# Weight loads of the recurrent stretch moved from SyncE's DMA queue to GpSimd's

## The chip, the cores and the metric

The kernel runs on one core of a Trainium2 chip. The metric is the device time of one launch in microseconds (us); lower is better. The engines are named as in the profile: PE (matmul), PEld (the weight load into PE), DVE (VectorE), ACT (ScalarE), POOL (GpSimd) and SP (SyncE, which here only issues DMAs). A name with a q behind it (SPq, ACTq) is the engine's DMA-issuing instructions.

## The reference, cut to what matters

One inference step of a two-layer decoder, for a prompt of 1024 tokens and 8 samples of 8 tokens, width 1024, all in float32:

```python
for i in range(DEPTH):                       # 2 layers
    h, gate = ada_norm(x, c, ...)            # RMS norm with shift, scale and gate from c
    o = stick_breaking(h) if i == 0 else rwkv7(h)
    x = x + gate * (o @ w_o)
    h, gate = ada_norm(x, c, ...)
    x = x + gate * (square(relu(h @ w_up)) @ w_down)     # hidden width 4096

# rwkv7: r, k, v = three 1024x1024 products; decay w, a, g by small low-rank products; then per head
def step(S, inp):
    sa = einsum('bhij,bhj->bhi', S, kk_t)
    S = S * w_t - sa * b_t + v_t * k_t
    return S, einsum('bhij,bhj->bhi', S, r_t)
```

## The kernel before

**Halves.** The 1088 tokens are two halves, A (576 columns, all prompt) and B (448 prompt columns and the 64 sample columns). A dense product of one half is the foreground; attention, and later the recurrence, is a background stream of generators whose steps are put between the matmuls (`step`, `behind`, `beside`). The order of the recurrent part is: first norm of the recurrent layer for A (`rw_norm`), `mixer_in(0)` with the products by `rw_w_r`, `rw_w_k` and `rw_w_v`; then for B the attention's `sb_w_o`, the first layer's MLP (`w_up`, `w_down` in eight blocks), `rw_norm` and `mixer_in(1)`; then for A `rw_w_o` and the last MLP; then the same for B.

**Weights.** `weight` brings one weight tile at a time: a DMA into the stage tile `wst` (three buffers; 512 KB, or 256 KB for `w_down`), a rounded copy `wh` by ACT (L350) and the remainder `wl` by DVE (L351), three buffers each. `dense` then runs three matmuls for each 128 rows (L364 to L366): `wh` by the high part of the operand, `wh` by its low part, `wl` by the high part. A load into `wst` waits until DVE has read the tile three loads earlier (L351). L347 is the line of that DMA. It goes to ACT's queue while the samples' attention runs (`sampling`), and to SP's queue otherwise.

**The recurrence.** For each half and each of eight pairs of heads, `rw_unit` (L1082 on) loads `k` and `r`, prepares the chunk matrices and stores them (`s_st`, `s_l`); on POOL it has the operations L1105 (`G`), L1108, L1119, L1120 (`a`) and L1130 (`AR`). `rw_lanes` loads `llt` (L1207), inverts small triangular blocks on DVE (L1216, L1218) and stores `s_tt` and `s_xn` (L1223, L1226). `rw_chain` then loads `st`, `tt`, `Lq`, `x` and `hv` (L1262 to L1274) and walks the chunks in two rows at once (`qc`, `invq`). `rw_out` normalises the result (POOL: L1465, L1482, L1498). Most stores of `rw_unit` and `rw_value` (`s_st`, `s_l`, `s_p`, `s_v`) go to ACT's queue; all loads go to SP's.

**Order.** The order of the instructions of each engine is set when the kernel is built: a scheduler plays the program through with times of its own, and each engine's queue gets the order that comes out. On the chip each queue runs in that order; an instruction whose semaphores are not there yet holds all behind it on its engine.

The rest of POOL's work in this part: the one-column copies `prod` (L552) of the attention's carry, the low parts `xlo` and `slo` of every other operand tile (L311), and, for B, the 64 sample columns of the norms (L302 to L304) and of the residual (L385).

Of the kernel before, what the change touches and what calls it, by code (L numbers as in the profile page):

```python
# [106 lines left out]
class Kern:  # L107
# [35 lines left out]
    def setup(self, ctx):  # L143
        nc, tc, I = self.nc, self.tc, self.I
        self.misc = ctx.enter_context(tc.tile_pool(name="misc", bufs=1))
        self.dram = ctx.enter_context(tc.tile_pool(name="scr", bufs=1, space=DRAM))
        cst = self.misc.tile([128, C_N], F32, name="cst")
        nc.sync.dma_start(cst, I["consts"])
        self.cst = cst
        self.ident = cst[:, C_ID:C_ID + 128]  # L150
        self.ones32 = self.misc.tile([128, 32], F32, name="ones32")
        nc.vector.memset(self.ones32, 1.0)
        self.sampling = False
        self.behind(iter(()))
        self.side = iter(())
        self.beside(iter(()), 0.0)
        self.eps = self.misc.tile([128, 1], F32, name="eps")
        nc.vector.memset(self.eps, EPS)
# [99 lines left out]
    def rms(self, x, pt, tmp, ps, tag, slot, rslot=None):  # L258

        for R in self.rms_steps(x, pt, tmp, ps, tag, slot, rslot):  # L260
            pass
        return R

    def rms_steps(self, x, pt, tmp, ps, tag, slot, rslot=None):
# [19 lines left out]
        nc.vector.tensor_mul(r, y, t)  # L284
        R = tmp.tile([128, W], F32, tag=rslot or slot, name="R", bufs=2 if rslot else None)
        for g in range(4):
            qb = ps.tile([128, 512], F32, tag=tag, name="rb")
            nc.tensor.matmul(qb[:, :w], self.cst[:, C_SELB + 128 * g:C_SELB + 128 * g + 128], r,
                             start=True, stop=True)
            self.copy(R[:, w * g:w * g + w], qb[:, :w])  # L290
        yield R

    def modulate(self, s, f, x, R, pt, t):

        nc = self.nc
        mod = self.mod[s]
        P, S = slice(0, pt.NP), slice(pt.NP, pt.W)
        nc.vector.scalar_tensor_tensor(t[:, P], x[f][:, P], mod[:, 8 + f, 0:1], R[:, P], ALU.mult,
                                       ALU.mult)
        if pt.NP < pt.W:  # L300
            ts = t[:, S].rearrange("p (b t) -> p b t", b=8)
            nc.gpsimd.tensor_mul(t[:, S], x[f][:, S], R[:, S])  # L302
            nc.gpsimd.tensor_mul(ts, ts, mod[:, 8 + f, 1:9].unsqueeze(2).to_broadcast([128, 8, 8]))
            nc.gpsimd.tensor_add(ts, ts, mod[:, f, 1:9].unsqueeze(2).to_broadcast([128, 8, 8]))  # L304
        return mod[:, f, 0:1]
# [35 lines left out]
    def weight(self, ap):  # L341

        nc = self.nc
        kt = ap.shape[1]
        st = self.wp.tile([128, kt, 128], F32, tag="wst", name="wst")
        q = nc.scalar if self.sampling else nc.sync
        q.dma_start(st, ap)  # L347
        wh = self.wp.tile([128, kt, 128], F32R, tag="wh", name="wh", bufs=WHL)
        wl = self.wp.tile([128, kt, 128], F32R, tag="wl", name="wl", bufs=WHL)
        nc.scalar.copy(wh, st)  # L350
        nc.vector.tensor_sub(wl, st, wh.bitcast(F32))  # L351
        return wh, wl

    def dense(self, w, mts, hi, lo, pt, ps, evac):

        nc = self.nc
        kt = len(hi)
        for m in mts:
            wh, wl = self.weight(w[m])
            for c0, n in pt.ch:  # L360
                q = ps.tile([128, 512], F32, tag="dps", name="dq")[:, :n]
                for k in range(kt):
                    h, l = hi[k][:, c0:c0 + n], lo[k][:, c0:c0 + n]
                    nc.tensor.matmul(q, wh[:, k, :], h, start=k == 0, stop=False)  # L364
                    nc.tensor.matmul(q, wh[:, k, :], l, start=False, stop=False)  # L365
                    nc.tensor.matmul(q, wl[:, k, :], h, start=False, stop=k == kt - 1)  # L366
                    self.step(n)
                evac(m, c0, n, q)
# [1203 lines left out]
    def rest(self, ctx, lp, hp, xp, tmp, PS):  # L1572
        nc, I = self.nc, self.I
        A, B = HALF
        rms = lambda x, pt: self.rms(x, pt, tmp, PS, "dps", "n", "R")
        dense = lambda w, parts, pt, evac: self.dense(w, range(NT), *parts, pt, PS, evac)
        norm = lambda s, x, R, pt: self.norm_split(s, x, R, pt, hp, tmp, "n")
        self.ready = set()

        def aside(*works, n=AS):  # L1580
            with ExitStack() as ctx:
                ps = self.psum(ctx, (("aux", n),))
                for w in works:
                    yield from w(ps)

        def second(ps):

            for self.RB in self.rms_steps(Passing(self, I["x"], B, tmp), B, tmp, ps, "aux", "n", "R"):
                yield
            self.hB = ([], [])  # L1590
            yield from self.norm_tiles(0, Passing(self, I["x"], B, tmp), self.RB, B, hp, tmp, "n",
                                       self.hB)


        self.load_c(tmp)
        self.load_params()
        self.load_x(A, xp)
        x = self.x
        R = rms(x, A)
        for _ in aside(lambda ps: self.ada_steps(0, ps, "aux", (0, 4, 1, 5, 2, 6, 3, 7)), n=BG):  # L1600
            pass
        self.att_setup(self.misc)
        self.xscr = self.dram.tile([NT, 128, T], F32, name="xscr")
        h = norm(0, x, R, A)
        self.behind(aside(second), 1 / 5)
        self.qkv(*h, A, tmp, PS)
        self.until(lambda: False)
        h = self.hB
        self.behind(self.background(), RATE)
        self.beside(itertools.chain(self.ada_steps(0, PS, "aux", range(8, 12)),  # L1610
                                    *(self.ada_steps(s, PS, "aux") for s in (1, 2, 3))), 40 / 180)
        self.qkv(*h, B, tmp, PS)
        self.beside(iter(()), 0.0)
        self.until(lambda: ("o", 0) in self.ready)
        self.beside(self.ahead(("o", 0), self.s_o, I["x"], A, hp, tmp), 1)
        self.beside(iter(()), 0.0)

        x, o = self.next
        dense(I["sb_w_o"], o, A, self.residual(0, x, A, tmp))
        self.show("x1", x, A)  # L1620
        R = rms(x, A)
        self.rw_setup(lp)
        self.ffn(1, x, *norm(1, x, R, A), A, hp, tmp, PS)
        self.show("x2", x, A)
        self.spill(x, A)
        self.until(lambda: ("o", 1) in self.ready)
        self.rw_late(ctx.enter_context(self.pool(name="lq", bufs=1)))
        self.ready.add("rw")
        R = rms(x, A)
        r = self.rw_norm(x, R, A, hp, tmp)  # L1630
        self.mixer_in(0, r, hp, tmp, PS, self.ahead(("o", 1), self.s_o, I["x"], B, hp, tmp))
        self.beside(iter(()), 0.0)
        x, o = self.next
        dense(I["sb_w_o"], o, B, self.residual(0, x, B, tmp))
        RB = rms(x, B)
        self.ffn(1, x, *norm(1, x, RB, B), B, hp, tmp, PS)
        self.show("x2", x, B)
        self.spill(x, B)
        R = rms(x, B)
        r = self.rw_norm(x, R, B, hp, tmp)  # L1640
        self.rw_shift()
        self.mixer_in(1, r, hp, tmp, PS, self.ahead(("y", 0), self.s_y, self.xscr, A, hp, tmp))
        self.until(lambda: ("y", 0) in self.ready)
        self.beside(iter(()), 0.0)
        x, y = self.next
        dense(I["rw_w_o"], y, A, self.residual(2, x, A, tmp))
        self.show("x3", x, A)
        R = rms(x, A)
        self.ffn(3, x, *norm(3, x, R, A), A, hp, tmp, PS)
        self.until(lambda: False)  # L1650
        with ExitStack() as ctx:
            xp = ctx.enter_context(self.pool(name="x2", bufs=8))
            xB = self.load_tiles(self.xscr, B, xp)
            y = ([], [])
            for _ in self.load_split(self.s_y, B, hp, tmp, y):
                pass
            dense(I["rw_w_o"], y, B, self.residual(2, xB, B, tmp))
            self.show("x3", xB, B)
            R = rms(xB, B)
            self.behind(self.final(x, A, tmp, PS))  # L1660
            self.ffn(3, xB, *norm(3, xB, R, B), B, hp, tmp, PS)
            self.until(lambda: False)
            for _ in self.final(xB, B, tmp, PS):
                pass
# [121 lines left out]
```

## Time and profile before

| what | value |
|---|---|
| median of 3 runs (lowest, highest) | 3655.77 us (3653.04, 3656.8) |
| the profiled execution | 3661.88 us, its span 3660.2 us |
| mean granted TensorE clock of the profiled execution | 0.972 |
| busy: PE, PEld, DVE, ACT, POOL | 95%, 76%, 64%, 44%, 18% of the span |
| DMA traffic | 634.45 MB, mean 173 GB/s |
| DMA queues' share of 16 engines | q1 45.1%, q10 7.9% |

In the profile, a line of waits reads: engine and line that waited, what it waited for, total us, how many times, the longest. A row of the table by stretches reads: from and to in us, the length, then busy us (and instruction count) of PE, PEld, DVE, ACT and POOL, the granted clock of TensorE as a part of full speed, the share of the DMA engines that was busy, and GB/s. A row of the timeline reads: start, length, engine, line, instruction, and in brackets the idle time before it and what ended it. A row of the chain of waits (the work that ended last, followed back) reads: start, length, what.

The loads of `rw_w_r` for A start at 1332.8 us, the last `w_down` loads of A's last MLP at 3150.6 us and after; so the part that the change touches lies at about 1330 to 3200 us of the span.

### The profile page before, as it was taken

The page shows a single profiled execution, that of the slowest core. Times are in us where ns is not written, and L with a number is a line of the kernel's source. Part 1 is how long each engine was busy: PE and PEld are TensorE (multiplying, and loading weights), DVE is VectorE, ACT ScalarE, POOL GpSimd, SP SyncE. Part 2 cuts the span into 40 slices and gives each one's busy share as a digit, 9 for nine tenths or more (in the row PEclk, how much of TensorE's full clock was granted, in tenths as well). Part 3 has the DMA queues.
Part 4 walks back from the last instruction along what each step waited for, and adds up shares of the span by engine and source line. Part 5 has one row for each costly group of instructions (what it writes and reads, how often), then busy time and mean ns, then how long its engine had stood idle before and what let it go on. Part 6 is the DMA issues. An engine that isn't in the chain of part 4 may idle for free.

```text
span 3660.2 us, 71034 instructions
## 1 busy us (share of the span) xinstructions
PE 3490.5 (95%) x26360; PEld 2764.7 (76%) x26360; DVE 2328.6 (64%) x4718; ACT 1601.2 (44%) x3341; POOL 669.3 (18%) x1180
## 2 busy tenths in 40 slices
PE   8999999899999998998899998998899999989998
PEld 6976667778888875876677776666798888868886
DVE  4457788785554555778855556766984666655444
ACT  4345566663333335644334445644433444433332
POOL 1223333230000001121312113121100111121111
PEclk9999999999999999999899998999999999999999
DMA  7475653319887785667354345667444444433332
GB/s 257 141 242 190 213 168 131 88 50 337 337 295 265 277 311 162 209 201 218 95 149 139 121 148 164 188 193 234 120 129 136 140 137 124 120 114 118 94 93 84
DMA packets 433003, 634.45 MB, mean 173 GB/s; under 512 B 144337, under 2 KB 244562, under 8 KB 432658
## 3 DMA queue, kind: packets, MB, share of 16 engines
q1 hardware_dynamic: 369394, 532.90, 45.1%
q10 hardware_dynamic: 63264, 97.02, 7.9%
q8 instruction: 209, 3.42, 0.4%
q14 instruction: 136, 1.11, 0.1%
HBM read 523.76 MB, written 106.01 MB: 172 GB/s over the span
## 4 chain that ended last, share of the span: by engine, by line
PE 44%; DVE 5%; DMA 3%; issue 1%; POOL 1%; ACT 1%; SPq 1%; ACTq 0%; DVEq 0%; POOLq 0%
PE dq L364 12%; PE dq L365 12%; PE dq L366 12%; PE qc L1335 1%; PE qc L1325 1%; PE qc L1344 1%; DMA s_v<-vt 1%; PE yq L1492 1%; DMA st<-s_st 0%; DVE lxn L1218 0%; PE qc L1339 0%; DVE wl L351 0%; DVE tm L1216 0%; PE s L1152 0%; PE qc L1348 0%
## 5 line engine op out<-in xcount | busy, mean ns | idle before, releaser
L350 ACT CAST wh<-wst 128x512 fp32r<-128x512 f32 (+1 forms) x512 | 424.6, 834 | 720.5 <-PE dq L365 606.3
L364 PE MATMUL dq<-hhi,wh 128*128 128x288 f32 (+1 forms) x2112 | 709.5, 337 | 11.2 <-ACT hhi L132 7.8
L365 PE MATMUL dq<-hlo,wh 128*128 128x288 f32 (+1 forms) x2112 | 703.6, 333 | 9.6 <-DVE hlo L332 9.6
L366 PE MATMUL dq<-hhi,wl 128*128 128x288 f32 (+1 forms) x2112 | 704.6, 334 | 0.2 <-DVE wl L351 0.2
L351 DVE TENSOR_TENSOR wl<-wst,wh 128x512 fp32r<-128x512 f32 (+1 forms) x512 | 499.4, 976 | 253.9 <-ACT wh L350 229.3
L364 PE MATMUL dq<-uh,wh 128*128 128x288 f32 (+1 forms) x1536 | 506.9, 335 | 2.9 <-DVE x L379 1.4
L365 PE MATMUL dq<-ul,wh 128*128 128x288 f32 (+1 forms) x1536 | 508.2, 331 | 0.0
L366 PE MATMUL dq<-uh,wl 128*128 128x288 f32 (+1 forms) x1536 | 505.5, 331 | 0.0
L364 PEld LDWEIGHTS dq<-hhi,wh 128*128 128x128 f32 x2112 | 399.9, 190 | 63.3 <-issue 20.4
L365 PEld LDWEIGHTS dq<-hlo,wh 128*128 128x128 f32 x2112 | 400.1, 189 | 49.3 <-issue 10.9
L366 PEld LDWEIGHTS dq<-hhi,wl 128*128 128x128 f32 x2112 | 399.7, 189 | 42.8 <-issue 12.3
L379 DVE SCALAR_TENSOR_TENSOR x<-dq,mod,x 128x288 f32<-128x288 f32 (+1 forms) x432 | 245.5, 569 | 231.4 <-PE dq L366 228.4
L364 PEld LDWEIGHTS dq<-uh,wh 128*128 128x128 f32 x1536 | 287.6, 188 | 52.5 <-issue 15.9
L554 DVE TENSOR_TENSOR_SCAN prod<-prod 128x256 f32<-128x256 f32 (+5 forms) x264 | 240.7, 913 | 121.6 <-ACT prod L545 86.8
L366 PEld LDWEIGHTS dq<-uh,wl 128*128 128x128 f32 x1536 | 288.0, 188 | 28.1 <-issue 4.2
L365 PEld LDWEIGHTS dq<-ul,wh 128*128 128x128 f32 x1536 | 288.3, 188 | 26.8 <-issue 5.3
L385 POOL TENSOR_TENSOR x<-x,rs 128x64 f32<-128x64 f32 x144 | 120.8, 839 | 605.1 <-DVE rs L382 591.4
L364 PE MATMUL dq<-xhi,wh 128*128 128x288 f32 (+1 forms) x576 | 204.5, 355 | 8.4 <-ACT xhi L132 5.8
L365 PE MATMUL dq<-xlo,wh 128*128 128x288 f32 (+1 forms) x576 | 199.0, 345 | 1.0 <-DVE xlo L311 0.9
L366 PE MATMUL dq<-xhi,wl 128*128 128x288 f32 (+1 forms) x576 | 197.6, 343 | 0.0
L555 DVE TENSOR_TENSOR beta<-beta,prod 128x256 f32<-128x256 f32 (+5 forms) x264 | 140.4, 535 | 29.5 <-POOL beta L600 9.0
L478 ACT CAST uh<-ut 128x288 fp32r<-128x288 f32 (+1 forms) x192 | 94.8, 495 | 131.3 <-DVE ut L476 130.5
(300 smaller groups left out, 6113.4 us busy)
## 6 DMA issues: line engine op xcount, KB each, us to landing
pagek<-cache_kT SPq DMA_DIRECT2D x128, 512.0 KB
pagev<-cache_v SPq DMA_DIRECT2D x128, 512.0 KB
adaw<-ada_w SPq DMA_DIRECT2D x192, 256.0 KB
wst<-w_up SPq DMA_DIRECT2D x96, 512.0 KB
wst<-w_down SPq DMA_DIRECT2D x192, 256.0 KB
st<-s_st SPq DMA_DIRECT2D x40, 672.0 KB
wst<-sb_w_qkv SPq DMA_DIRECT2D x48, 512.0 KB
wst<-w_up ACTq DMA_DIRECT2D x32, 512.0 KB
```

The lines of the kernel that those rows point to most:

```text
L350: nc.scalar.copy(wh, st)
L351: nc.vector.tensor_sub(wl, st, wh.bitcast(F32))
L364: nc.tensor.matmul(q, wh[:, k, :], h, start=k == 0, stop=False)
L365: nc.tensor.matmul(q, wh[:, k, :], l, start=False, stop=False)
L366: nc.tensor.matmul(q, wl[:, k, :], h, start=False, stop=k == kt - 1)
L379: nc.vector.scalar_tensor_tensor(xs, q[:, :np_], g, xs, ALU.mult, ALU.add)
L385: nc.gpsimd.tensor_add(xv, xv, t)
L478: nc.scalar.copy(a, t[:, :n])
L554: nc.vector.tensor_tensor_scan(r, r, r, 1.0 if carry is None else carry, ALU.mult, ALU.bypass)
L555: nc.vector.tensor_mul(beta[:, :w], beta[:, :w], p[:, 1:w + 1])
L1325: nc.tensor.matmul(qc[R[hd], 0:64], st[:, hd, cc, :], hv[hd][:, cc, :], start=True, stop=True)
L1335: nc.tensor.matmul(qc[r, 64:128], tt[r, cc, :], xs[r, :], start=True, stop=True)
```

## The change

A second flag, `recurring`, is set from the recurrent layer's first norm to the end of A's last MLP. While it is set, `weight` issues its DMA from POOL instead of SP.

```diff
-        self.sampling = False
+        self.sampling = self.recurring = False
...
-        q = nc.scalar if self.sampling else nc.sync
+        q = nc.scalar if self.sampling else nc.gpsimd if self.recurring else nc.sync
         q.dma_start(st, ap)
...
         self.ready.add("rw")
+        self.recurring = True
         R = rms(x, A)
         r = self.rw_norm(x, R, A, hp, tmp)
...
         self.ffn(3, x, *norm(3, x, R, A), A, hp, tmp, PS)
         self.until(lambda: False)
+        self.recurring = False
```

These are 256 loads: 2 x 24 of `rw_w_r`, `rw_w_k` and `rw_w_v`, 8 of `sb_w_o`, 8 of `rw_w_o`, and twice 32 of `w_up` and 64 of `w_down`. POOL's queue grows from 1161 to 1417 instructions, by these 256 and nothing else. The scheduler's play-through changes with it, so that the order on the other engines changes too, without a change in what they compute. Three places follow, in which a row is line, instruction, written tile and read tile, shape, and how many stand together; rows with - stand only before, with + only now.

SP, where the second half's chains begin: `s_xn` and `s_tt` are the last stores of the inverses, `st` and `tt` the first loads of `rw_chain`.

```order
 L1226 DMA s_xn<-lxn 8x32x32
 L1223 DMA s_tt<-llt 8x32x32 x2
-L347 DMA wst<-w_up 128x1024 x2
 L1262 DMA st<-s_st_9669 128x7x192
 L1265 DMA tt<-s_tt 128x192
```

The two loads of `w_up` that stood ahead of the first chain load are no longer on SP.

POOL, at the end of the samples' attention, where the first weight loads of the recurrent layer now stand: `prod` (L552) is the copied carry of an attention step.

```order
 L550 MEMSET prod 128x1
+L347 DMA wst<-rw_w_r 128x1024
 L702 TENSOR_TENSOR beta<-beta,cst 128x8
-L552 COPY prod<-prod 128x1 x6
+L552 COPY prod<-prod 128x1 x3
+L347 DMA wst<-rw_w_r 128x1024
+L552 COPY prod<-prod 128x1
+L347 DMA wst<-rw_w_r 128x1024 x2
+L552 COPY prod<-prod 128x1
+L347 DMA wst<-rw_w_r 128x1024
+L552 COPY prod<-prod 128x1
```

Five weight loads stand between copies that stood together before.

POOL, in `mixer_in(0)`, around one `rw_unit` (L1119 to L1105 of the next one).

```order
 L1119 TENSOR_SCALAR a<-a 128x576
 L1108 COPY gend<-G 128x9
 L1130 TENSOR_TENSOR AR<-r,G 128x576
 L1120 TENSOR_TENSOR a<-a,Gi 128x576
+L347 DMA wst<-rw_w_k 128x1024 x2
 L1105 MEMSET G 128x9
+L347 DMA wst<-rw_w_k 128x1024
```

The next unit's first POOL operation now stands behind two weight loads, and its others behind a third.

## The prediction

> **What bounds the kernel.** I read the busy shares first, then the stretches of the touched part, then who waits there, then the chain of waits and SP's timeline at the places where PE stood.
>
> ```profile
> PE 3490.5 (95%) x26360; PEld 2764.7 (76%) x26360; DVE 2328.6 (64%) x4718; ACT 1601.2 (44%) x3341; POOL 669.3 (18%) x1180
> ```
>
> PE is busy 95% of the span, so the most that any queue could give over the whole kernel is the 170 us in which PE stands. The change acts from 1330 to about 3200 us; by stretches (PE, PEld, DVE, ACT, POOL, clock, DMA share, GB/s):
>
> ```profile
> 1330.00:1400.00 70.00, 53.47 (x512) 35.58 (x511) 46.42 (x81) 37.53 (x68) 13.17 (x22) 0.87 0.82 302
> 1400.00:1500.00 100.00, 96.11 (x606) 74.74 (x605) 51.22 (x82) 48.44 (x84) 10.63 (x8) 0.95 0.48 153
> 1500.00:1600.00 100.00, 97.66 (x744) 78.57 (x743) 74.62 (x147) 59.38 (x115) 17.88 (x19) 0.98 0.68 221
> 1600.00:1740.00 140.00, 116.20 (x771) 92.82 (x771) 116.34 (x281) 54.41 (x110) 28.18 (x25) 0.91 0.71 212
> 1740.00:1830.00 90.00, 74.69 (x392) 58.16 (x391) 74.98 (x175) 32.84 (x62) 32.83 (x46) 0.87 0.32 91
> 1830.00:2230.00 400.00, 399.80 (x2946) 300.57 (x2945) 220.91 (x542) 166.83 (x420) 65.72 (x100) 1.00 0.45 135
> 2230.00:2300.00 70.00, 58.17 (x573) 41.23 (x572) 54.80 (x138) 45.14 (x115) 31.20 (x73) 0.80 0.71 213
> 2300.00:2450.00 150.00, 147.55 (x883) 96.72 (x882) 106.81 (x227) 84.30 (x158) 27.39 (x30) 1.00 0.58 188
> 2450.00:2640.00 190.00, 160.10 (x1048) 123.94 (x1048) 145.80 (x330) 79.66 (x144) 34.13 (x50) 0.90 0.62 186
> 2640.00:2800.00 160.00, 156.06 (x1276) 147.93 (x1275) 108.87 (x265) 56.82 (x132) 5.56 (x12) 0.97 0.46 129
> 2800.00:3190.00 390.00, 389.62 (x3698) 328.80 (x3697) 257.21 (x645) 159.73 (x457) 44.13 (x62) 1.00 0.43 129
> 3190.00:3280.00 90.00, 79.90 (x506) 65.93 (x505) 50.90 (x93) 30.75 (x49) 21.88 (x27) 0.96 0.41 138
> sum 1950.00, PE 1829.33 PEld 1444.99 DVE 1308.90 ACT 855.82 POOL 332.70; mean PE 152.44 PEld 120.42 DVE 109.08 ACT 71.32 POOL 27.72
> ```
>
> Two things are to be seen. In the two MLP stretches, 1830 to 2230 and 2800 to 3190, PE is busy 789.42 of 790 us: nothing is to be had there, only lost. All that could be gained lies in the other stretches, 1950 - 1829.33 = 120.7 us of idle PE. And where PE idles the granted clock is lower: PE's busy time times the missing clock, summed over the rows (116.20 x 0.09 = 10.5 and 160.10 x 0.10 = 16.0 are the larger ones), is 69 us. I count 69/120.7 = 0.57 us of clock for each idle us that comes or goes, a proportion read off these rows and not a law.
>
> Who waits in 1330 to 3190 (total, times, longest):
>
> ```profile
> SPq L347 <- DVE wl L351: 332.4, 120, 9.2
> ACT wh L350 <- PE dq L365: 186.5, 123, 8.8
> ACT wh L350 <- DMA wst<-w_up: 9.4, 2, 6.9
> PE invq L1294 <- DMA tt<-s_tt: 5.8, 2, 3.3
> PE invq L1285 <- DMA x<-s_xn: 3.9, 2, 3.5
> PE gq L1004 <- DMA gb<-rw_g: 3.4, 3, 1.7
> ```
>
> SP waits 332.4 us at weight loads for their stage buffer, with everything behind them on its queue; that is what the change takes off SP. The weights themselves are early: the cast to `wh` waits 123 times for PE to give a buffer back and twice for a `w_up` load. The waits of PE for a DMA are all for operands of the chains and the gate, and they are small.
>
> **The change part by part.** SP loses 256 issues and their waits. Where does that reach PE? At three places the chain of waits, or PE's own wait, runs through an operand load close behind weight loads. The start of the second half's chains, in the chain of waits:
>
> ```profile
> 2756.27 0.38 SPq L347
> 2756.75 0.51 SPq L347
> 2757.36 7.15 DMA st<-s_st
> ...
> 2767.71 4.88 DMA st<-s_st
> ```
>
> Two `w_up` issues stand on the path for 0.89 us, and the `st` load behind them takes 7.15 us against 4.88 for one without weights directly ahead. Without them: 0.89 + 2.27 = 3.2 us (between 0 and the 3.5 us that PE stood for `x` there). The other two, from the chain, SP's timeline and PE's:
>
> ```profile
> 1698.42 5.79 DMA x<-x
> 1704.59 2.33 DMA x<-x
> 2254.41 5.94 DMA tt<-s_tt
> ```
> ```profile
> st<-s_st SPq DMA_DIRECT2D x40, 672.0 KB
> 1687.94 1.89 SPq L347 DMA_DIRECT2D wst<-sb_w_o  x2
> 1693.52 5.23 SPq L433 DMA_DIRECT2D x<-x  x4
> 1705.98 1.33 PE L140 MATMUL vq<-cst,dn 128*128 128x128 f32 x5 [6.54 <-ACT dn L132]
> 2251.43 0.35 SPq L347 DMA_DIRECT2D wst<-rw_w_r  x1
> 2253.05 0.56 SPq L1262 DMA_DIRECT2D st<-s_st  x1
> ```
>
> At 1693 four loads of `x` follow two of `sb_w_o`; the slow one is 5.79 - 2.33 = 3.5 us longer than the later one. I take half, 1.7 (0 to 3.5), because the four loads also share the engines among themselves. At 2254 `tt` has 672 KB of `st` and a `rw_w_r` load just ahead; of PE's 3.3 us wait I take 1.5 (0 to 3.3), since `st` stays where it is. The gate's `gb` waited 3.4 us in three pieces, some behind weight loads: 1.0 (0 to 3.4). Together 3.2 + 1.7 + 1.5 + 1.0 = 7.4 us of idle PE (0 to 13.7), and with the clock 7.4 x 1.57 = 11.6 (0 to 21.5).
>
> What hides the rest of SP's 332.4 us: in the MLP stretches PE itself, with no idle time left; elsewhere DVE, busy 116.34 of 140 and 145.80 of 190 us, which sets the pace of the inverses and units whatever the queue does.
>
> POOL gains 256 issues, each with its wait for DVE's `wl`, and what stands behind them on POOL waits too. No row shows a DMA issued by POOL, so its price is bounded by POOL's small operations and SP's issue:
>
> ```profile
> L385 POOL TENSOR_TENSOR x<-x,rs 128x64 f32<-128x64 f32 x144 | 120.8, 839 | 605.1 <-DVE rs L382 591.4 <-PE lq L1090 6.2 <-PE dq L366 4.1
> L1120 POOL TENSOR_TENSOR a<-a,Gi 128x576 f32<-128x576 f32 (+1 forms) x16 | 23.3, 1455 | 0.4
> 1784.60 4.68 POOL L302 TENSOR_TENSOR hf<-x,R 128x64 f32<-128x64 f32 x1
> 1790.66 0.32 POOL L302 TENSOR_TENSOR hf<-x,R 128x64 f32<-128x64 f32 x1
> ```
>
> The casts of the weight tiles, of the whole part and of the stretch 1830 to 2230, count the loads:
>
> ```profile
> L350 ACT CAST wh<-wst 128x512 fp32r<-128x512 f32 (+1 forms) x254 | 211.1, 834 | 259.0 <-PE dq L365 186.5 <-issue 21.8 <-PE dq L366 10.5
> L350 ACT CAST wh<-wst 128x512 fp32r<-128x512 f32 (+1 forms) x80 | 61.3, 771 | 90.8 <-PE dq L365 63.5 <-issue 10.7 <-DMA s_tt<-llt 4.4
> ```
>
> The same operation on 64 columns takes 0.32 us when POOL runs freely, 0.84 in the mean of the 144 residual adds, and 4.68 once, beside a DVE at work. I take 0.84 us for an issue (0.32 to 4.68): 215 us on top of POOL's 332.7, 28% of the part. That alone is off the path. On the path are two things. At the end of the samples' attention five loads now stand between the carry copies; four copies that are behind one, at 0.84 us at worst 3.4; the loads come free shortly before the copies are due, so I take 1.0. In the units, POOL's operations stand behind loads that wait for `wl`: 332.4/120 = 2.8 us where a load waits, which 120 of 254 loads do. For 16 units that is 16 x 0.47 x 2.8 = 21 us if all of it lay on the path, and 0 if DVE's own work covers it. The chain in the unit stretches runs over DVE and the DMAs, scarcely over POOL, so I am near the lower end and take 1.3. Together 2.3, with the clock 3.6 (0 to 38).
>
> The sample columns' norm (L302 to L304) has no load among its operations. The late loads that could hurt PE, those of the MLPs, have a lead: PE takes 400/80 = 5 us a tile there, and with three `wst` and three `wh` a load can go out up to six tiles, 30 us, ahead of its use, against a wait of at most 9.2 us and an issue of 0.84: no cost while that lead lasts. If it ran out, the cast would be late first, then the matmul.
>
> Sum: -11.6 + 3.6 = -8.0 us. Against the profiled execution, 3661.88 us (6.1 above the median; its span 3660.2), this is 3654; on the median of 3655.77, 3648.
>
> **The rivals.** *No change.* The four operand loads are slow because of the bytes in flight and not because of their place in a queue: DMA engines are busy 0.71 in both stretches of `x` and `tt`. Then only the 0.89 us of issue is gained, 1.4 with the clock, less POOL's 3.6: 3658, within 0.2% (7.3 us), which is about what a measurement of this kernel tells from no change. The Trainium skill says this in "DMA: Bandwidth & Descriptors", section "Issuing engines are not separate DMA queues": issuing from several engines saves only the sequencer's issue time. The trace neither bears it out nor refutes it, since here all weights and loads are on one queue.
>
> *Slower by POOL's order.* If the 21 us of the units and the attention's 3.4 lie on the path, the loss is 24.4 x 1.57 = 38, the net +27: 3682. It decides from 12 us of new idle PE on ((11.6 + 7.3)/1.57), that is, half of it. For it speaks that POOL's operations precede DVE's next ones in each unit; against it, that the scheduler puts the loads where their buffer comes free.
>
> *Slower by a starved POOL.* If every load took POOL 4.68 us, 80 loads and POOL's own 65.72 us would need 440 us in the stretch of 400 and about 418 in that of 390: 40 + 28 us, 3724. It decides once an issue takes over (400 - 65.7)/80 = 4.2 us. "SBUF — State Buffer" of the Trainium skill, section "SBUF: two separate sides", names such a mechanism: a DVE operation in a two-port mode locks GpSimd out while it should write descriptors, 3.1 us instead of 0.62 in its example. The row of 4.68 us agrees in kind; that most rows are under 1 us speaks against it as the rule.
>
> **How the numbers follow.** The forecast, faster by more than 0.2%: 0.45. No change: 0.26. Slower by POOL's order 0.23 and by starvation 0.06, together 0.29. The new order of all engines alone can move some microseconds either way, which is why the middle is not larger. The range, 3627 to 3689, goes from the full 21.5 us of gain (3634) to the full price of POOL's order (3682), with 7 us at both ends for the new order; the forecast's own is 3634 to 3648.
>
> **What would show it.** Right: PE's waits for `tt`, `x` and `gb` shrink; the first `st` of the second half takes about 5 us; PE's idle time in the stretches of 1600 to 1740 and 2230 to 2300 falls; the MLP stretches stay at 100%. Wrong: POOL operations of the units, or the carry copies, wait for `wl`; casts wait for `wst` loads and then PE for casts in the MLPs; rows of POOL's L347 of several us.

## The result: 0.96% slower

The changed kernel takes 3692.1 us (median of 4 runs, 3690.99 to 3693.91) against 3654.4 us: the ratio is 1.0096, 95% interval 1.0081 to 1.0111. The forecast was 3648 us, the range 3627 to 3689. The profiled execution has a span of 3689.4 us. Every ratio in this document leaves out executions more than 1.5% above the fastest of the same kernel; there were two, one of e8 (3733.6 us) and one of e11 (9313.9 us).

The profile after, first the busy time of each engine and two rows of the DMA queues (queue, kind: packets, MB, share of the 16 engines):

```profile
PE 3504.1 (95%) x26360; PEld 2776.6 (75%) x26360; DVE 2327.8 (63%) x4718; ACT 1602.7 (43%) x3342; POOL 804.4 (22%) x1436
...
q1 hardware_dynamic: 332530, 432.22, 36.6%
q0 software_dynamic: 28672, 100.68, 8.6%
```

The 256 loads are a queue of their own, q0, and cost POOL 804.4 - 669.3 = 135 us. The costliest of them, by groups (count, busy, mean ns, idle time ahead and what ended it), and their issue to landing in us:

```profile
L347 POOL DMA_DIRECT2D wst<-w_down x128 | 71.7, 560 | 456.3 <-DVE wl L351 310.5 <-DVE hv L134 24.3 <-DVE hv L1354 17.6
L347 POOL DMA_DIRECT2D wst<-w_up x64 | 35.7, 558 | 120.4 <-DVE wl L351 68.9 <-DVE hv L134 11.2 <-DVE lxn L1218 9.9
...
wst<-w_up POOLq DMA_DIRECT2D x64, 512.0 KB, 3.6
wst<-w_down POOLq DMA_DIRECT2D x128, 256.0 KB, 3.1
```

An issue takes 0.56 us, and the load lands 3 to 4 us later. The waits after, in the same part (1330 to 3230 us):

```profile
POOL wst L347 <- DVE wl L351: 590.7, 110, 20.2
ACT wh L350 <- PE dq L365: 235.3, 146, 7.1
PE invq L1294 <- DMA tt<-s_tt: 5.3, 2, 4.6
PE gq L1004 <- DMA gb<-rw_g: 4.9, 2, 2.6
PE invq L1285 <- DMA x<-s_xn: 2.7, 2, 2.2
```

POOL now has SP's wait for `wl`, and longer. The casts still wait for PE, so weights are early, as before. And PE's small waits for the chains' operands, where the gain was to come from, have hardly changed.

**Where the time went.** The casts of the weight tiles (L350) come in the same order in both kernels. Their start after minus their start before says how late the foreground is at that place:

| first cast of | before, us | after minus before |
|---|---|---|
| B's first MLP | 1753.8 | -8.0 |
| B's `rw_w_r` | 2244.5 | -14.0 |
| A's `rw_w_o` | 2516.8 | -9.2 |
| A's last MLP | 2594.9 | -9.9 |
| its third block | 2743.3 | +14.8 |
| B's `rw_w_o` | 3215.5 | +6.6 |
| first `w_down` of B's last MLP | 3301.2 | +28.0 |

So the kernel does run ahead at first, by up to 14 us. It loses 25 us at the beginning of A's last MLP, and 21 us at B's `rw_w_o`. The two places in the table by stretches (columns as in the prediction's; the first place in two rows, up to the third tile of `w_down` and on to the third block), before:

```profile
2594.86:2669.26 74.40, 60.15 (x494) 52.48 (x493) 63.62 (x152) 34.65 (x68) 9.66 (x17) 0.89 0.45 119
...
2669.26:2743.34 74.08, 74.08 (x583) 72.78 (x582) 64.03 (x161) 23.22 (x48) 4.25 (x9) 1.00 0.39 118
...
3215.48:3244.59 29.11, 29.11 (x156) 25.08 (x156) 12.69 (x20) 8.87 (x13) 5.26 (x5) 1.00 0.56 192
```

and after, with nearly all of the MLP between them:

```profile
2584.98:2671.62 86.64, 67.50 (x532) 59.03 (x532) 81.49 (x210) 36.77 (x71) 13.67 (x25) 0.80 0.37 103
...
2671.62:2758.19 86.57, 80.62 (x623) 75.81 (x621) 67.68 (x168) 28.30 (x59) 13.40 (x24) 0.98 0.48 133
...
2796.10:3197.52 401.42, 401.38 (x3832) 339.01 (x3831) 255.61 (x636) 164.41 (x468) 71.33 (x117) 1.00 0.43 127
...
3222.12:3271.77 49.65, 39.47 (x216) 28.30 (x215) 21.91 (x43) 11.52 (x17) 9.20 (x10) 0.90 0.42 134
```

The MLP is full (PE 401.38 of 401.42 us). The first place loses 12 us in each of its rows. In the first, DVE is busy 81.49 of 86.64 us with 210 instructions, where it was 63.62 us with 152. In the second, PE has 40 instructions more and stands 6 us, 4.8 of them for steps of a unit (`PE s L1152`), where it did not stand before. Of the 25 us, 11 come back in the tiles right behind, where the second half's chains begin (37.91 us instead of 49.28, with 258 PE instructions instead of 399: work put off again). The second place has 60 PE instructions more and 10 us of idle PE. What DVE does more in the first row of the first place, by groups, before and after:

```profile
L1218 DVE TENSOR_TENSOR lxn<-lxn,tm 128x240 f32<-128x240 f32 (+11 forms) x12 | 3.7, 309 | 0.0
L1216 DVE TENSOR_TENSOR tm<-llt,lxn 128x240 f32<-128x240 f32 (+11 forms) x12 | 3.6, 303 | 0.0
```
```profile
L1216 DVE TENSOR_TENSOR tm<-llt,lxn 128x31 f32<-128x31 f32 (+15 forms) x31 | 10.8, 350 | 4.7 <-DMA s_st<-AR 4.4
L1218 DVE TENSOR_TENSOR lxn<-lxn,tm 128x31 f32<-128x31 f32 (+15 forms) x31 | 10.5, 339 | 0.2
```

These are the inverses of `rw_lanes`: 62 of them instead of 24 stand beside A's last norm. PE waits there for DVE's part of the norm, which it did not before:

```profile
PE rb L288 <- DVE rv L284: 8.2, 1, 8.2
```

At the second place, the chain of waits after shows the last output of the second half with nothing beside it:

```profile
3250.15 0.46 ACT yT L1495
3250.68 0.61 POOL yT L1498
3251.31 0.30 DVE yT L1501
3251.63 0.32 SPq L1502
...
3255.80 5.53 DMA t<-s_y
3261.36 0.63 ACT shi L132
3262.03 1.65 PE dq L364 x3
```

B's `rw_w_o` needs that `y`; PE stands for 9.3 us (`PE dq L364 <- ACT shi`). In the kernel before the last store of `y` went out at 3218.5 us, beside matmuls, and PE waits for nothing there.

Both are matters of order, and the built order says the same without any time. Of the 592 PE instructions of the units, 424 stand ahead of A's `rw_w_o` before and 390 after: one unit, 34 instructions, has moved behind it. Ahead of the first weight of A's MLP stand 227 of 310 DVE instructions of the inverses before, and 196 after. Ahead of B's `rw_w_o` stood all 320 PE instructions of the outputs; now 12 of them stand behind it. Did the queue do this on the chip, or the order that the scheduler made of it?

### The profile page after: what moved, and what is told of

It reads as the page before. It is cut to its first block, busy times and chain, and to the rows that moved or that the text cites. A ratio compares the mean times of both kernels' runs of the same rounds, so it can differ in the third digit from the quotient of the medians.

```text
span 3689.4 us, 71256 instructions
## 1 busy us (share of the span) xinstructions
PE 3504.1 (95%) x26360; PEld 2776.6 (75%) x26360; DVE 2327.8 (63%) x4718; ACT 1602.7 (43%) x3342; POOL 804.4 (22%) x1436
## 3 DMA queue, kind: packets, MB, share of 16 engines
q1 hardware_dynamic: 332530, 432.22, 36.6%
## 4 chain that ended last, share of the span: by engine, by line
PE 81%; DVE 8%; DMA 4%; issue 2%; ACT 2%; SPq 2%; POOL 1%; ACTq 0%; DVEq 0%; POOLq 0%
PE dq L364 20%; PE dq L366 19%; PE dq L365 19%; PE tq L140 2%; PE o L623 2%; PE zs L687 2%; PE os L745 2%; PE adaq L246 2%; PE z L589 1%; PE qc L1335 1%; PE qc L1325 1%; PE qc L1344 1%; DVE lxn L1218 1%; DVE tm L1216 1%; PE lq L1090 1%
## 5 line engine op out<-in xcount | busy, mean ns | idle before, releaser
L350 ACT CAST wh<-wst 128x512 fp32r<-128x512 f32 (+1 forms) x512 | 424.5, 834 | 751.3 <-PE dq L365 637.2
L364 PE MATMUL dq<-hhi,wh 128*128 128x288 f32 (+1 forms) x2112 | 712.1, 338 | 6.4 <-ACT hhi L132 5.7
L364 PE MATMUL dq<-uh,wh 128*128 128x288 f32 (+1 forms) x1536 | 509.8, 336 | 2.5 <-ACT uh L478 1.1
L364 PEld LDWEIGHTS dq<-hhi,wh 128*128 128x128 f32 x2112 | 400.7, 190 | 59.0 <-issue 20.2
L364 PEld LDWEIGHTS dq<-uh,wh 128*128 128x128 f32 x1536 | 288.6, 188 | 51.7 <-issue 14.6
L364 PE MATMUL dq<-xhi,wh 128*128 128x288 f32 (+1 forms) x576 | 207.1, 360 | 7.6 <-ACT xhi L132 7.3
L347 POOL DMA_DIRECT2D wst<-w_down x128 | 71.7, 560 | 456.3 <-DVE wl L351 310.5
```

## The experiments

Each ratio is against the kernel before, run beside it on the same chip.

**Order and queue apart.** The trace of the program is the same for both queues, so the kernel can be built once to read an order, and a second time with that order laid down as edges between neighbours on each engine (issue order alone, no semaphore):

```diff
+        if order:
+            here = {i.name: i for i in nc.cur_bb.bb.instructions}
+            for e in PINNED:
+                names = [n for n in order[e] if n in here and here[n].engine == e]
+                for a, b in zip(names, names[1:]):
+                    tc.add_manual_dep(here[b], a, mybir.DependencyInfo(
+                        mybir.DependencyClass.NoSync, mybir.DependencyReason.DATA), reason="order")
...
+    order = order_of(traced(arrays, False))
+    nc = traced(arrays, True, order)
```

`traced(arrays, on_pool, order)` builds the kernel with `recurring` set or not. The moved loads alone are free to stand where the scheduler puts them. As built, the queues of PE, DVE and ACT are then, instruction for instruction, those of the kernel whose order was laid down; the old order laid down with the loads on SP was not run by itself. The old order with the loads on POOL:

> All 256 loads on POOL's queue as in the changed kernel, but PE, DVE, ACT, SP and POOL's other operations keep the order of the kernel before, word for word. Theory 'order' (the loss is the new order of the other engines: A's norm beside larger inverses, and the second half's chains ending behind A's last MLP): both losses are gone and the 10 us gained up to the end of B's first MLP stay, so 3640 to 3650 us, ratio 0.996 to 0.999; the last store of y before 3225 us. Theory 'queue' (POOL's loads wait for wl and hold its unit, norm and output operations on the chip): still 20 to 40 us slower than before, 3675 to 3695 us, ratio 1.006 or more.

Measured: 1.0014 (1.0005 to 1.0022), 3662.9 us: the loss is gone, but the expected gain is not there, so that the number lies outside both ranges. The other way round, `order_of(traced(arrays, True))` and `traced(arrays, False, order)`, the new order with all loads on SP:

> No load on POOL: all on SP's queue as before, but PE, DVE, ACT, POOL and SP's other DMAs stand in the order of the changed kernel. Theory 'order': the loss of 25 us around A's last norm and of 20 us at B's rw_w_o come with it and the gain of 10 us does not, so 3690 to 3705 us, ratio 1.010 to 1.014. Theory 'queue': about the kernel before, 3650 to 3662 us, ratio 0.999 to 1.002.

Measured: 1.0102 (1.0085 to 1.0118), 3693.3 us, as 'order' has it. So the loss comes without a single load on POOL, and with all 256 on it it does not come. The row of the norm in this kernel is that of the changed one:

```profile
2582.78:2670.27 87.49, 66.54 (x556) 58.11 (x554) 81.74 (x210) 36.70 (x71) 10.45 (x19) 0.84 0.34 96
```

The order theory missed one thing: the gain of the first part also comes with the order, not with the queue. The lag of the foreground, as in the table above, for these and the later kernels:

| kernel | B's first MLP | B's `rw_w_r` | A's `rw_w_o` | A's last MLP | its third block | its seventh | B's `rw_w_o` | B's last MLP |
|---|---|---|---|---|---|---|---|---|
| changed kernel | -8.0 | -14.0 | -9.2 | -9.9 | +14.8 | +10.6 | +6.6 | +28.0 |
| e1, old order, POOL | -5.5 | -0.7 | +2.4 | +1.4 | +2.4 | +1.1 | +1.4 | +1.9 |
| e2, new order, SP | -17.9 | -22.9 | -13.4 | -12.1 | +10.7 | +14.1 | +10.9 | +31.9 |
| e5, first piece new | -17.6 | -18.2 | -16.8 | -16.6 | -16.3 | -18.4 | -18.5 | -18.1 |
| e6, second piece new | -6.8 | -8.2 | -2.4 | -1.0 | +22.6 | +26.1 | +25.3 | +24.8 |
| e7, third piece new | -7.1 | -6.2 | -4.1 | -4.4 | -6.1 | -7.7 | -10.3 | +10.0 |
| e9, eight loads | -10.1 | -18.1 | -12.6 | -7.3 | +13.8 | +9.0 | +1.9 | +22.7 |
| e10, late at the norm | -2.6 | -1.4 | +5.5 | -5.5 | +16.3 | +21.7 | +20.9 | +21.2 |
| e11, late in the mixer | -5.1 | -4.6 | -0.5 | +28.1 | +27.3 | +23.3 | +23.1 | +23.6 |
| e12, tail caught up | -3.4 | -2.9 | -3.6 | -4.3 | -4.3 | -7.8 | +3.5 | +4.0 |

These are single profiled executions; that of the kernel before is 6 us above its median, that of e5 6 us below, so that e5 is -18 us here and -8 in the timed runs. The kernels with an unchanged order in the first column (e1, e6, e7 and e10 to e12) lie at -2.6 to -7.1 there, so differences under about 5 us of this table say nothing.

**Part of the flag.** Two kernels with orders of their own. First the flag cleared after B's first MLP:

```diff
         self.spill(x, B)
+        self.recurring = False
         R = rms(x, B)
```

> The flag is cleared at the end of B's first MLP, so 128 + 8 fewer: loads of rw_w_r, rw_w_k and rw_w_v for A, sb_w_o and the first MLP for B go to POOL, those of the second part to SP. The order is built anew; in it the second half's chains end at the same place in A's last MLP as before. Theory 'order': the gain of the first part stays, neither loss comes, 3640 to 3650 us, ratio 0.996 to 0.999. Theory 'queue' with the place in the second part: the same 3640 to 3650; so this run tells only whether the gain of the first part holds to the end.

Measured: 1.0061 (1.0048 to 1.0074). Both theories missed it. The foreground is 16 us early at B's `rw_w_r`, and 14 us late at the third block of A's MLP. The units stand where they stood before, at A's `rw_w_o` and at its MLP (424 and 526 PE instructions); so it is not the unit that is late. The loss has no single place: against the kernel before, the foreground loses 9, 5 and 5 us in B's products by `rw_w_r`, `rw_w_k` and `rw_w_v`, 5 us in A's `rw_w_o`, and 8 us from there to the third block. PE's largest wait in the stretch of 2451 to 2545 us, for the copies of `rw_value`, explains little of it, before and in this kernel:

```profile
PE vq L140 <- ACT dn L132: 7.9, 3, 4.6
```
```profile
PE vq L140 <- ACT dn L132: 10.6, 3, 4.4
```

I have not taken this order apart; why it loses is open. Then the flag set only from B's recurrent norm on (the line moved down to there):

> The flag is set only from B's recurrent norm on, so the loads of rw_w_r, rw_w_k and rw_w_v for B, rw_w_o and the last MLP for A go to POOL. In its own new order the second half's last chain and output stand at 82.1 to 82.3% of the foreground's columns, inside A's last MLP (82.35% is its end; before 81.8 to 82.1, changed kernel 82.7 to 82.9). Theory 'order': no exposed tail at B's rw_w_o, so at most the other loss of up to 25 us less some of it that comes back inside the MLP: 3650 to 3670 us, ratio 0.999 to 1.004. Theory 'queue': both losses as in the changed kernel and no gain of the first part: 3690 to 3705 us, ratio 1.010 to 1.014.

Measured: 1.0059 (1.0046 to 1.0072), between the two expectations. The lag is -6.0 us at A's last MLP, +13.2 at its third block, +13.2 at B's `rw_w_o` and +16.4 at B's MLP: the loss at the norm comes, the exposed tail scarcely. The place was right, the size above the range of 'order' (up to 1.004).

**The new order in three pieces.** The order as built is one list over all engines. These kernels take it up to a cut from one build, and what is left from the other:

```diff
+PIECES = [("new", "mlp_1B"), ("old", None)]
...
+        for which, until in PIECES:
+            for n, _ in orders[which]:
+                if until and n == at[until]:
+                    break
+                if n not in done and n not in moved:
+                    done.add(n)
+                    yield n
```

Their line numbers are 3 or 4 higher than the kernel's. e5 has this list, e6 `("old", "mlp_1B"), ("new", "block_3A2"), ("old", None)`, e7 `("old", "block_3A2"), ("new", None)`.

> All loads on SP's queue. Every engine stands in the changed kernel's order up to the first matmul of B's first MLP (about 1755 us), and in the old order behind it. Theory 'three pieces' (the new order gains about 20 us in this piece, and loses in the two behind it, each by itself): the gain stays, 3632 to 3645 us, ratio 0.994 to 0.998. Theory 'deferred' (the first piece is early only because work was put off, which has to be done later): the gain is given back by 2700 us, 3650 to 3662 us, ratio 0.999 to 1.002.

Measured: 0.9977 (0.9967 to 0.9986): 8 us faster, and kept to the end.

> All loads on SP's queue. Old order up to the first matmul of B's first MLP, the changed kernel's order from there to the third block of A's last MLP (about 2745 us), old order behind that. In the new order one unit of the second half more (34 of its PE instructions) stands behind A's last norm instead of ahead of it. Theory 'three pieces': this piece holds the first loss, 25 to 30 us, 3675 to 3690 us, ratio 1.006 to 1.010. Theory 'deferred': 3650 to 3665 us, since this piece lost only what the first had won, ratio 0.999 to 1.003.

Measured: 1.0085 (1.0069 to 1.0101), 31 us, nearly all of it between the first weight and the third block of A's last MLP.

> All loads on SP's queue. Old order up to the third block of A's last MLP, the changed kernel's order from there on; all units stand ahead of the cut in both, only the chains and outputs move: 12 output matmuls that stood inside A's MLP stand behind it. Theory 'three pieces': the exposed tail costs its 20 us by itself, 3670 to 3682 us, ratio 1.004 to 1.008. Theory 'deferred': the tail is late only because the chains began late; with an old beginning it is hidden, 3652 to 3662 us, ratio 0.999 to 1.002.

Measured: 1.0045 (1.0028 to 1.0062), 16 us: the foreground runs 4 us ahead inside the MLP and loses 20 at B's `rw_w_o`.

The pieces add up: -0.23 + 0.85 + 0.45 = 1.07%, against 1.02% of the whole new order. As ratios all three lie in the ranges given for 'three pieces', the first at its small end, and outside those for 'deferred'; in us, e5 and e6 lie above theirs, beside a kernel before of 3659.4 in that call. The fourth run of the group, e5's order with the loads on POOL (`traced(arrays, True, order)`):

> As the kernel with the new first piece, but with all 256 loads on POOL's queue as in the changed kernel. The old order with the loads on POOL was 0.14% (5 us) slower than before; so, if the queue's price and the order's add up, 5 us above the same order with the loads on SP: 3637 to 3650 us and faster than before under 'three pieces', 3655 to 3667 us under 'deferred'.

Measured: 0.9984 (0.9972 to 0.9996): faster than before, as 'three pieces' has it, though its 3653.2 us lie 3 us above the range. That is the third pair with one order and two queues. POOL's is 0.14% slower in the old order, 0.07% in this one, and 0.06% faster in the new one (1.0096 against 1.0102, in different calls): between 2 us faster and 5 us slower. Only the 0.14% is clear of the noise.

**How little it takes, and how lateness is paid.** First, only the 8 loads of `sb_w_o` for B on POOL:

```diff
+        self.recurring = True
         dense(I["sb_w_o"], o, B, self.residual(0, x, B, tmp))
+        self.recurring = False
```

> Only the 8 loads of sb_w_o for B go to POOL's queue, the other 248 stay on SP's; the order is built anew. These 8 give nearly the changed kernel's order in the second part: 12 output matmuls behind A's last MLP, one unit of the second half more behind A's rw_w_o, 196 DVE operations of the inverses ahead of A's last norm (kernel before 227). Theory 'order': about the same loss as with 256 loads, 3680 to 3695 us, ratio 1.006 to 1.011. Theory 'queue': 8 of 256 loads, so at most a thirtieth of the change's loss, 3653 to 3658 us, ratio 0.999 to 1.001.

Measured: 1.0078 (1.0060 to 1.0096), 3684.8 us, at the places of the changed kernel (its row in the table). (The flag is set nowhere else.) 3% of the loads bring four fifths of the loss.

Then the second piece in two, `("old", "out_A"), ("new", "block_3A2"), ("old", None)`:

> Loads on SP. Old order up to the first matmul of A's rw_w_o, the changed kernel's from there to the third block of A's last MLP, old behind it. In it the work is late only from rw_w_o on: 196 instead of 227 inverse operations of DVE stand ahead of the MLP's first weight. Theory 'DVE in A's norm' (31 inverse operations of about 0.37 us, 11 to 12 us, and a unit's own stand beside the norm, which DVE then paces): the loss of the second piece comes nearly whole, 15 to 28 us, ratio 1.004 to 1.008. Rival 'mixer' (the second piece loses in B's mixer, ahead of rw_w_o): ratio 0.999 to 1.002.

Measured: 1.0067 (1.0040 to 1.0093), about what 'DVE in A's norm' has. Its norm:

```profile
2589.38:2676.36 86.98, 67.56 (x556) 58.74 (x554) 80.85 (x207) 36.80 (x71) 10.63 (x19) 0.84 0.34 96
```

And `("old", "mixer_B"), ("new", "out_A"), ("old", None)`:

> Loads on SP. The changed kernel's order only from B's first rw_w_r matmul to A's rw_w_o, old order ahead and behind. The unit that is late in the mixer is caught up in one go at rw_w_o, so that 227 inverse operations stand ahead of A's MLP again. Theory 'DVE in A's norm': no loss left, ratio 0.999 to 1.002. Rival 'mixer': most of the 31 us, ratio 1.005 to 1.009.

Measured: 1.0092 (1.0072 to 1.0112). The number is the rival's, the place is not. There is no loss in the mixer (-4.6 us at `rw_w_r`, -0.5 at `rw_w_o`), and none at the norm, which takes 73.59 us. All of it lies between the first and the fifth tile of A's `rw_w_o`, before and in this kernel:

```profile
2516.84:2558.74 41.90, 37.01 (x245) 29.66 (x244) 25.76 (x59) 16.42 (x34) 4.79 (x8) 0.92 0.83 263
```
```profile
2516.36:2586.82 70.46, 50.96 (x339) 38.94 (x336) 42.55 (x101) 23.73 (x49) 7.86 (x16) 0.81 0.65 197
```

This is where the late unit is made up in one go. I had taken that for free; its steps run from engine to engine with no matmuls of the foreground between them (PE's waits and its timeline, this kernel):

```profile
PE kb L1068 <- DVE kv L1064: 7.5, 1, 7.5
PE bkq L1184 <- ACT L L1173: 4.5, 1, 4.5
PE s L1156 <- DVE BK L1140: 3.3, 1, 3.3
...
2545.07 4.26 PE L1156 MATMUL s<-AR,BK 64*128 64x128 f32 x32 [3.35 <-DVE BK L1140]
2553.81 1.34 PE L1184 MATMUL bkq<-cst,BK 64*128 64x64 f32 x15 [4.48 <-ACT L L1173]
```

So my expectation was wrong in its premise: one unit late has its price at either place where it was made up, 24 us at the norm (e10; interval 15 to 34) or 34 at `rw_w_o` (e11; 26 to 41). These intervals overlap, so which place is dearer is not shown.

Last, the exposed tail, `("old", "block_3A2"), ("new", "block_3A6"), ("old", None)`:

> Loads on SP. As the kernel whose third piece alone is new, but back to the old order from the seventh block of A's last MLP (about 3060 us), so that the chains run late through blocks 3 to 6 and the outputs end inside the MLP again. Theory 'exposed tail' (chains that run late inside the MLP cost nothing; what costs is their end, with nothing beside it): the 0.45% are gone, 3650 to 3660 us, ratio 0.998 to 1.001. Rival 'late chains' (the lateness itself costs): ratio 1.003 to 1.006.

Measured: 1.0034 (1.0020 to 1.0047), nearer to 'late chains' than to 'exposed tail'. The tail is gone (3.5 us late at B's `rw_w_o`, 4.0 behind it), but the `w_up` part of the block where the chains catch up takes 45.50 us instead of 33.68, before and in this kernel:

```profile
3056.76:3090.44 33.68, 33.68 (x331) 26.75 (x329) 26.57 (x62) 14.18 (x37) 7.69 (x11) 1.00 0.56 174
```
```profile
3048.99:3094.49 45.50, 40.28 (x395) 31.86 (x393) 30.84 (x80) 18.07 (x52) 9.31 (x13) 0.92 0.46 137
```

64 PE instructions more in that part, 5.2 us of idle PE, and a lower clock. In this kernel the chains that were put off are paid for where they catch up, 12 us here against about 20 behind the MLP.

e5 beats both kernels: 0.23% faster than before, 1.2% faster than the changed one (0.9977/1.0096), with all loads on SP. If they are to be on POOL, e8's order is the one, 0.16% faster than before.

## Why the prediction was wrong

**The step that failed** is the one sentence on the order: "The new order of all engines alone can move some microseconds either way", with 7 us at both ends of the range. Measured by itself (e2) it moves 37 us (3693.3 against 3656.2): -8, +31 and +16 us in three pieces. I had shown three places where the order moved and priced the loads there, but not what the loads' move did to the order elsewhere: one unit behind A's `rw_w_o`, 31 inverses beside A's norm and 12 output matmuls behind the MLP could be counted from the built orders beforehand.

**The gain of SP's queue, 11.6 us,** did not come. In e1, where only the queue differs, PE's waits for those operands shrank, in the same part:

```profile
PE invq L1294 <- DMA tt<-s_tt: 5.1, 2, 2.9
PE invq L1285 <- DMA x<-s_xn: 2.5, 3, 1.4
PE gq L1004 <- DMA gb<-rw_g: 1.8, 1, 1.8
```

From 5.8, 3.9 and 3.4 us, so by 3.7. The stretch in which the second half's chains begin (from the first `w_up` to the third `w_down` tile of the third block of A's last MLP) is 2.2 us shorter, before and in e1:

```profile
2743.34:2792.62 49.28, 45.34 (x399) 42.68 (x398) 17.98 (x40) 16.80 (x44) 0.00 (x0) 0.90 0.57 150
```
```profile
2745.76:2792.83 47.07, 43.83 (x394) 41.27 (x393) 18.23 (x40) 16.84 (x44) 3.65 (x9) 0.93 0.59 156
```

The other pair of one order, e5 (loads on SP) and e8 (on POOL), says how much of this is the queue. The stretch, in e5 and in e8:

```profile
2727.02:2774.60 47.58, 44.38 (x399) 41.68 (x398) 17.98 (x40) 16.82 (x44) 0.00 (x0) 0.93 0.59 156
```
```profile
2734.04:2779.91 45.87, 43.23 (x394) 40.65 (x393) 18.14 (x40) 16.80 (x44) 3.63 (x9) 0.93 0.61 158
```

It is shorter again, by 1.7 us, but the three waits sum to 10.6 us in e5 and 11.7 in e8: they have not shrunk. And e11, with its loads on SP and the old order here, takes 46.55 us for the stretch. So about 2 us repeat, within the scatter of single executions, and that SP's queue cost PE the 7.4 us of idle time is not shown. Nothing of it reached the end: from A's fifth `rw_w_r` tile to the first `w_down` of B's last MLP e1's profile takes 1883.86 us, the one before 1884.41, and the timed runs are 5 us slower. The rule cited for 'No change' ("DMA: Bandwidth & Descriptors", section "Issuing engines are not separate DMA queues", of the Trainium skill) is the nearest to what the queue alone did.

**POOL's price.** An issue takes 0.56 us, not 0.84 (bounds 0.32 to 4.68). The gain and the whole price on POOL together come to between -2 and +5 us, against the -8.0 forecast. That the MLPs lose nothing to the loads was right. 'Starved' is out: no group of L347 on POOL has a mean over 0.59 us, and its longest single issue took 1.07 us. What "SBUF — State Buffer" of the Trainium skill, section "SBUF: two separate sides", says of GpSimd locked out while DVE runs an operation in a two-port mode does not show in these issues, with DVE busy 63% of the span. Whether any of DVE's operations beside them ran in such a mode, the trace does not say.

**'Slower by POOL's order',** at 3682, had the sign and came near the number, but not the cause: POOL's operations behind loads are in e1 too, which is 5 us slower, and not in e2, which is 37.

The chance of 0.29 for slower held two mechanisms of POOL and nothing for the order of the other engines, which did it.

What stays open: what the new order of the first piece saves (8 us), whether SP's queue cost PE anything, and what e3's order does wrong.

## What to carry to other kernels

Where a scheduler sets the order from its own times, a change of one queue is two changes, and the second can be many times the first: here at most 5 us and 37 us, and 8 loads of 256 were enough for most of it. Pin the old order to price the change, and pin the new one without the change to price the order. To judge a new order beforehand, count at the places where the foreground gives no cover (a norm, an output product) how much background work stands ahead of them and how much behind: here one unit on the wrong side cost 24 us, a dozen output matmuls with the chains ahead of them 16, and making up for them in one go 34 and 12. The count finds such places but does not price a whole order: e3 has the unit counts of the kernel before at A's `rw_w_o` and its MLP and is 22 us slower, e5 has them too and is 8 us faster.

## What the hardware showed

A load issued by POOL takes its engine 0.56 us (mean of 128 `w_down` loads of 256 KB, and the same, 0.558, for 64 of 512 KB), lands 3.1 and 3.6 us after its issue, and counts as POOL's busy time; the issues of the same line on SP's queue took 0.33 us each. All 256 run as a queue of their own (8.6% of the engines' time, SP's fell from 45.1 to 36.6%), with no difference over 0.14% of the kernel's time to SP's queue in the same order.
